# Attention on one core: one cell in five gets its exp on VectorE from 16-bit integer bits and a quadratic, with q, k and v cast and transposed by DMA, in a planned fixed order

## The chip, the cores and the metric

One core of a Trainium2 chip. The time is the device time of that core in microseconds (us). Most executions of one kernel agree within 0.3%. Each run has a state, fast or slow. A kernel's run carries runs of the kernel before on the same chip, so that ratios are taken within one chip.

Engines in the profile: PE is TensorE's matmuls, PEld its weight loads, DVE is VectorE, ACT is ScalarE, POOL is GpSimd, SP is the engine that only issues DMAs. A name with a q (SPq, POOLq) is that engine's issuing side.

## The reference

```python
# q [8, 8, 1024, 64], k and v [8, 2, 1024, 64], float32, all normal x 0.1
for g in range(2):                              # 4 query heads share a k, v head
    scores = (1/8) * q_group @ k_group.transpose(0, 1, 3, 2)
    attn = exp(scores - max(scores))
    attn = attn / (sum(attn) + 1e-08)
    output[:, 4*g : 4*g + 4] = attn @ v_group
```

The scores are tiny, so both kernels leave the maximum out. The sum comes from a column of ones beside v. Work is counted in cells of 128 keys by 512 queries: 8 batches x 8 heads x 2 query blocks x 8 key blocks are 1024 cells.

## The kernel before

Three cells make a wave: three score matmuls fill a PSUM tile of 1536 columns, and one ACTIVATE takes the exp of all. q and k are transposed by PE, and DVE copies the transposes out.

```python
def score_wave(gw, qT, kT):
    ...
    sps = spool.tile([128, CPERW, QBS], FP32, name="spsum")      # CPERW = 3, bufs=2
    for slot, gc in enumerate(cells):
        nc.tensor.matmul(sps[:, slot, :], lhsT=kT[b][g][side][:, c, :],
                         rhs=qT[(b, pair)][...], start=True, stop=True)
    pt = pT_pool.tile([128, CPERW, QBS], BF16, name="pt")
    nc.scalar.activation(out=pt[:, 0:n, :], in_=sps[:, 0:n, :], func=AF.Exp, scale=scale)
    return pt

def output_block(b, pair, side, qb, pts, vt):
    ...                          # 4 x 8 matmuls of pt by v and its column of ones
    nc.vector.reciprocal(out=rec, in_=ops[:, :, D])
    nc.vector.tensor_tensor(out=ost, in0=ops[:, :, 0:D], in1=rec..., op=ALU.mult)
    ...                          # DMA to out
```

The softmax here doesn't subtract the row's maximum and nothing guards it: scores larger than these inputs give would overflow.

## Time and profile before

| | before |
|---|---|
| time | 480.44 us, median of 2 runs (479.61 to 481.26) |
| ACT busy | 460.2 us of a span of 480.1 (96%) |
| PE busy / DVE busy / POOL busy | 443.3 / 129.3 / 141.1 us |
| granted PE clock, mean | 0.998 |

A high busy share does not make a bound by itself; who waits for whom does. The prediction below reads that from the groups, the chain of waits and the spacing of instructions, with their lines. One view that it only counts with is that of the DMA queues (packets, MB, share of 16 engines' span):

```profile
q1 hardware_dynamic: 102656, 25.18, 24.8%
q0 software_dynamic: 7168, 16.79, 11.1%
```

### The profile page before, as it was taken

The numbers are of one execution on the slowest core, as the hardware profiler recorded it, in microseconds if no ns is written. First come the engines' busy times: TensorE is split into PE (matmuls) and PEld (weight loads), VectorE is DVE, ScalarE is ACT, GpSimd is POOL, SyncE is SP. The second block draws the span as 40 slices with busy tenths as digits, with TensorE's granted clock in tenths as the row PEclk, the third lists the DMA queues.
The fourth block names the chain that finished last, engine by engine and source line by source line (L and its number), as shares of the span: only waits on it lengthen the run. The fifth ranks groups of instructions, "written<-read, shape, count | busy, mean of one in ns | idle before, by whom it ended". The sixth has DMA issues, their size and how long they took to land.

```text
span 480.1 us, 13304 instructions
## 1 busy us (share of the span) xinstructions
PE 443.3 (92%) x5632; PEld 282.6 (59%) x5632; DVE 129.3 (27%) x400; ACT 460.2 (96%) x343; POOL 141.1 (29%) x198
## 2 busy tenths in 40 slices
PE   2999999999999999999999999999999998988895
PEld 1566666666666666666565656656565555555553
DVE  3332233232242323222241312313222111111112
ACT  1699999999999999999999999999999999999996
POOL 9993056128047111830138010111100111101011
PEclk9999999999999999999999999999999999999999
DMA  7997356138157122842148121211212111111111
GB/s 177 218 227 182 79 142 169 45 90 219 35 125 198 47 55 58 197 109 58 35 115 206 34 56 46 67 34 35 56 45 58 40 39 35 46 34 34 46 34 45
DMA packets 109883, 42.82 MB, mean 89 GB/s; under 512 B 105728, under 2 KB 105728, under 8 KB 109824
## 3 DMA queue, kind: packets, MB, share of 16 engines
q1 hardware_dynamic: 102656, 25.18, 24.8%
q0 software_dynamic: 7168, 16.79, 11.1%
q8 instruction: 44, 0.72, 0.6%
q14 instruction: 15, 0.12, 0.1%
HBM read 25.17 MB, written 16.78 MB: 87 GB/s over the span
## 4 chain that ended last, share of the span: by engine, by line
ACT 72%; PE 21%; issue 3%; POOL 1%; DMA 1%; DVE 1%; POOLq 0%
ACT pt L191 72%; PE spsum L183 13%; PE opsum L204 6%; PE tpsum L107 2%; POOL qstage L87 1%; DMA qstage<-in_q_dram 1%; DVE ost L216 0%; DVE xT L111 0%; DVE rec L214 0%; POOL ident masks.py:199 0%; POOL ident masks.py:197 0%; POOLq masks.py:199 0%; POOLq L277 0%
## 5 line engine op out<-in xcount | busy, mean ns | idle before, releaser
L191 ACT ACTIVATE pt<-spsum 128x1536 bf16<-128x1536 f32 x342 | 458.9, 1706 | 14.6 <-PE spsum L183 14.6
L183 PE MATMUL spsum<-xT 128*128 128x512 bf16 x1024 | 278.2, 380 | 23.5 <-ACT pt L191 19.0
L204 PEld LDWEIGHTS <-pt 128*128 128x128 bf16 x4096 | 174.0, 98 | 75.9 <-DVE ost L216 16.9
L204 PE MATMUL opsum<-vstage,pt 128*128 128x65 bf16 x4096 | 191.1, 195 | 1.1 <-DVE ost L216 1.0
L183 PEld LDWEIGHTS <-xT 128*128 128x128 bf16 x1024 | 98.5, 97 | 94.2 <-issue 35.8
L222 POOL DMA_DIRECT2D out_dram<-ost x64 | 48.3, 755 | 316.1 <-DVE ost L216 283.6
L214 DVE RECIPROCAL rec<-opsum 128x4 f32<-128x4 f32 x128 | 23.4, 183 | 309.2 <-PE opsum L204 300.4
L87 POOL DMA_DIRECT2D qstage<-in_q_dram x128 | 92.2, 723 | 18.4 <-PE tpsum L107 12.8
L216 DVE TENSOR_TENSOR ost<-opsum,rec 128x256 f32<-128x256 f32 x128 | 53.8, 421 | 3.7 <-DVE rec L214 0.2
L111 DVE COPY xT<-tpsum 128x1024 bf16<-128x1024 bf16 x64 | 43.6, 681 | 32.9 <-PE tpsum L107 20.7
L107 PE MATMUL tpsum<-ident,kstage 128*128 128x128 bf16 x256 | 28.5, 226 | 5.4 <-DMA kstage<-in_k_dram 5.3
L107 PE MATMUL tpsum<-ident,qstage 128*128 128x128 bf16 x256 | 27.4, 225 | 3.3 <-DVE xT L111 1.6
L107 PEld LDWEIGHTS <-kstage 128*128 128x128 bf16 x256 | 18.9, 101 | 14.0 <-issue 5.7
L107 PEld LDWEIGHTS <-qstage 128*128 128x128 bf16 x256 | 18.6, 101 | 9.8 <-issue 2.8
L77 DVE MEMSET kstage<- 128x192 f32 x64 | 13.5, 218 | 2.3 <-PE tpsum L107 0.9
L191 ACT ACT_TABLE_LOAD x1 | 1.3, 1283 | 0.7 <-PEq L277 0.7
L96 DVE MEMSET vstage<- 128x8 f32 x16 | 0.9, 65 | 0.0
masks.py:199 POOL TENSOR_SCALAR_AFFINE_SELECT ident<-ident 128x128 bf16<-128x128 bf16 x1 | 0.3, 307 | 0.1
masks.py:197 POOL MEMSET ident<- 128x128 bf16 x1 | 0.2, 205 | 0.3 <-POOLq L277 0.3
L277 POOL MEMSET const-float32-0.0<- 128x1 f32 x1 | 0.1, 99 | 0.2 <-issue 0.2
L277 POOL MEMSET const-bfloat16-1.0<- 128x1 bf16 x1 | 0.1, 102 | 0.0
L277 POOL MEMSET const-uint8-127<- 128x1 uint8 x1 | 0.1, 102 | 0.0
(1 smaller groups left out, 0.1 us busy)
## 6 DMA issues: line engine op xcount, KB each, us to landing
qstage<-in_q_dram POOLq DMA_DIRECT2D x128, 64.0 KB, 3.7
qstage<-in_q_dram SPq DMA_DIRECT2D x128, 64.0 KB, 3.4
out_dram<-ost SPq DMA_DIRECT2D x64, 128.0 KB, 1.9
out_dram<-ost POOLq DMA_DIRECT2D x64, 128.0 KB, 2.3
kstage<-in_k_dram SPq DMA_DIRECT2D x64, 64.0 KB, 2.7
vstage<-in_v_dram SPq DMA_DIRECT2D x16, 256.0 KB, 3.1
```

What stands on the lines that cost most here:

```text
L77: nc.vector.memset(ks[:, 0::2, :], 0.0)
L87: eng.dma_start(out=qstage[sc][:, 2 * j : 2 * j + 2, :], in_=q[b, 2 * j : 2 * j + 2].rearrange("h (sc p) d -> sc p h d", p=128)[sc],)
L96: nc.vector.memset(vs[:, :, D], 1.0)
L107: nc.tensor.transpose(tp[:, sc, :], _hi16(stages[sc])[:, lo : lo + 2, :], ident)
L111: nc.vector.tensor_copy(out=dst, in_=tp)
L183: nc.tensor.matmul(sps[:, slot, :], lhsT=kT[b][g][side][:, c, :], rhs=qT[(b, pair)][:, qb * NQS : (qb + 1) * NQS, :], start=True, stop=True,)
L191: nc.scalar.activation(out=pt[:, 0:n, :], in_=sps[:, 0:n, :], func=AF.Exp, scale=scale)
L204: nc.tensor.matmul(ops[:, qs, :], lhsT=pts[gc // CPERW][:, gc % CPERW, qs * 128 : (qs + 1) * 128], rhs=_hi16(vt[b][g][:, c, :]), start=(c ...
L214: nc.vector.reciprocal(out=rec, in_=ops[:, :, D])
L216: nc.vector.tensor_tensor(out=ost, in0=ops[:, :, 0:D], in1=rec.unsqueeze(2).to_broadcast([128, NQS, D]), op=ALU.mult,)
L222: (nc.gpsimd if (qb + side) % 2 else nc.sync).dma_start(out=out[b, h].rearrange("(qs p) d -> p qs d", p=128)[:, qb * NQS : (qb + 1) * NQS, :],
L277: nc = _bacc.Bacc("TRN2", target_bir_lowering=False, num_devices=1)
```

## The change

ACT was the bound, so the change takes work from it. Four things are done together.

1. 194 of the 1024 cells go to DVE. A copy out of PSUM scales the score and adds 127 x 256, into a 16-bit integer. Its bits, shifted right by one, are those of a bf16 near exp; a quadratic in the low 8 bits corrects it. That is one step per cell and five steps for each group of four cells.
2. The other cells stay on ACT in pieces of two cells (1024 columns), not three, as PSUM banks are now needed for DVE's cells.
3. q and k are cast to bf16 by a DMA from DRAM to DRAM, issued by GpSimd, and read back by transposing DMAs that SP issues. GpSimd casts v, and copies k's halves into place.
4. A small simulation orders all instructions, with durations as its constants; no scheduler moves them.

```diff
+def make_plan(nj, nkc):
+    QK, PV, EXP, P1, NORM = 0.214, 0.142, 0.925, 0.665, 0.64
+    CHAIN = (0.60, 0.60, 1.08, 0.60, 1.08)
+    LIVE_A, LIVE_D, PENDING = 24, 7, 8
+    ...              # always takes the op that can start first; a cell goes to DVE when
+    ...              # a DVE bank is free before an ACT tile, with at most 8 pending
+            if pending < PENDING and (cur or live["D"] < LIVE_D):
+                td = max(pe, min(bank))
...
+def cast(key, src):
+    scr = scr_pool.tile([S, G * D], BF16, name="scr")        # in DRAM, bufs=4
+    nc.gpsimd.dma_start(out=scr..., in_=src...)
+    scratch[key] = scr
+def transpose(key, dst, n):
+    nc.sync.dma_start_transpose(out=dst[:, rows], in_=scratch[key][rows, :])
...
+# exp_bits, one cell, PSUM -> pd (uint16):   pd = score * bits_scale + 256*127
+# exp_curve, a group of four cells (2048 columns):
+#   z = pd & 0xFF            tensor_scalar
+#   y = z * A/512 + B/2      tensor_scalar, f16
+#   y = z * y                tensor_tensor
+#   z = pd >> 1              tensor_scalar
+#   pd = z + y               tensor_tensor, read as bf16
...
+            at(t0 - 24.0, cast, ("k", b), k[b])
+                at(t0 - 12.0 + 0.7 * n, transpose_k, b, n)
+                at(t0 - 5.0 + g, place_k, b, g)
...
+                at(max(tj - 21.0, -1.0), cast, ("q", b, j), q[b, j::NPAIR])
+                at(tj - 7.0 + 0.7 * n, transpose_q, b, j, n)
```

t0 and tj are the planned first use of a batch or a pair of heads, in us.

## The prediction

> **What bounds the kernel now.** I read the busy shares first, then the costliest groups, then the chain of waits, and last the timeline of each engine, for the spacing of its instructions. First the page's first part, and the stretches of the run.
>
> ```profile
> PE 443.3 (92%) x5632; PEld 282.6 (59%) x5632; DVE 129.3 (27%) x400; ACT 460.2 (96%) x343; POOL 141.1 (29%) x198
> ...
> 220.00:320.00 100.00, 95.31 (x1228) 60.87 (x1228) 26.78 (x81) 100.00 (x75) 22.05 (x30) 1.00 0.29 74
> ```
>
> PE and ACT both look full. Over 100 us of the middle (busy us of PE, weight load, DVE, ACT, POOL, then clock, DMA share, GB/s) ACT is busy for exactly 100. Who waits for whom decides between them:
>
> ```profile
> L191 ACT ACTIVATE pt<-spsum 128x1536 bf16<-128x1536 f32 x342 | 458.9, 1706 | 14.6 <-PE spsum L183 14.6
> L183 PE MATMUL spsum<-xT 128*128 128x512 bf16 x1024 | 278.2, 380 | 23.5 <-ACT pt L191 19.0
> L204 PE MATMUL opsum<-vstage,pt 128*128 128x65 bf16 x4096 | 191.1, 195 | 1.1 <-DVE ost L216 1.0
> ...
> ACT 72%; PE 21%; issue 3%; POOL 1%; DMA 1%; DVE 1%; POOLq 0%
> ```
>
> ACT idles 14.6 us behind the score matmuls in the whole run, 11.8 of them in one piece at the start, while PE waits for ACT all through. The kernel is ACT's exp over 1024 cells (a cell is 128 keys by 512 queries), plus a start and an end. Spacing, from the timeline of each engine (start, length):
>
> ```profile
> 228.88 12.47 ACT L191 ACTIVATE pt<-spsum 128x1536 bf16<-128x1536 f32 x9
> ...
> 232.00 0.81 PE L183 MATMUL spsum<-xT 128*128 128x512 bf16 x3 [0.27 <-ACT pt L191]
> 232.64 0.73 PE L204 MATMUL opsum<-vstage,pt 128*128 128x65 bf16 x17
> ...
> 11.92 2.72 PE L183 MATMUL spsum<-xT 128*128 128x512 bf16 x6 [0.78 <-DVE xT L111]
> ...
> 231.76 0.18 DVE L214 RECIPROCAL rec<-opsum 128x4 f32<-128x4 f32 x1 [3.35 <-PE opsum L204]
> 231.98 0.42 DVE L216 TENSOR_TENSOR ost<-opsum,rec 128x256 f32<-128x256 f32 x1
> ```
>
> - ACT: nine exps last 12.47 us; less one length of 1.71, over 8, they start every 1.345 us. The records overlap, so the mean length of 1706 ns is not the cost. 342 x 1.344 is 460 us of the 480.
> - PE: three score matmuls take 0.81, the last one 0.38, so they start every 0.215 us. Seventeen output matmuls take 0.73, the last 0.195: every 0.0335 us. PE's own need is 1024 x 0.215 + 4096 x 0.0335 = 220 + 137 = 357 us, not the 443 "busy". At the start six take 2.72: about 0.427 apart, half speed, up to about 20 us.
> - DVE: a reciprocal and the multiply after it take 0.22 + 0.42 = 0.64 us, 128 times: 82 us.
>
> **What the Trainium skill says.**
> - "ScalarE: Activation LUTs", What ACT_TABLE_LOAD costs: an ACTIVATE with immediate scale and bias takes 186 ns + 0.833 ns per element, and neighbours overlap by about 93. That makes 1373 ns between starts at 1536 elements; this trace has 1345. Keeping the slope, the fixed part is 1345 - 1280 = 65 ns, so an exp of 1024 should come every 853 + 65 = 0.918 us.
> - "VectorE: DVE Perf Modes", The perf-mode tier table: at 2048 elements of 16 bits in SBUF, a single-source operation takes 693 ns, tensor_tensor 1224; an fp32 PSUM source runs at one element per cycle. The trace has only the last kind: 0.42 us for 256 elements is 267 ns at 0.96 GHz plus 0.155.
> - "SBUF — State Buffer", Who interferes with whom: VectorE in a two-port mode and GpSimd exclude each other for a whole instruction, and a two-input VectorE instruction excludes GpSimd's reads. The kernel before cannot show it.
> - "TensorE: Matmul & The Clock Gate", What you observe: the first matmuls go at half speed. The 0.427 against 0.215 us agrees.
>
> **The change, part by part.** I counted instructions in the built program.
>
> *Exp leaves ACT.* 830 cells stay, as 415 exps of 1024; 194 go to DVE. ACT: 415 x 0.918 = 381 us, 79 less. Smaller pieces cost it: 277 pieces of 1536 would need 372. It also needs a quick PE. The old records give the round trip: the exp ends about 1.09 us after its start when not overlapped (1.45 less 512 x 0.833 = 1.02, plus 0.07 until PE starts), two matmuls 0.215 + 0.38, 0.04 to ACT: about 1.72. Two exps last 1.836. The slack is 0.11 us, less than one cell of output matmuls (4 x 0.0335 = 0.134), so I expect small gaps, 5 to 10 us in all: about 388.
>
> *DVE gets it.* Per group of four cells: 4 copies out of PSUM (512 elements, fp32 to 16 bits): 533 + 155 = 0.69 alone, some 0.66 where neighbours overlap: 2.64 us. Then three single-source steps and two tensor_tensor over 2048. The skill's lengths would be 0.69 and 1.22, the change's own planning constants are 0.60 and 1.08. Those constants look measured: 0.64 for the reciprocal and multiply and 0.214 for a score matmul both match the old trace. I lean to them, but each step waits for the one before: 0.63 and 1.12. Group: 2.64 + 3 x 0.63 + 2 x 1.12 = 6.77 us; 194 / 4 = 48.5 groups: 328. With the normalising, 82, DVE needs **410 us** (403 with the constants; 430 with the skill's lengths, 2.64 + 2.07 + 2.44 = 7.15 a group).
>
> *PE.* 512 transposes in the loop go (56 us busy in the groups, though pipelined); 16 stay at the start. 357 us of need remains.
>
> *Data.* Loads now go through a cast to DRAM by the GpSimd queue and a transposing DMA by the SP queue, issued some 21 and 7 us ahead. The old hardware queue had 102,656 packets in 24.8% of 16 engines' span: 0.248 x 480 x 16 / 102,656 = 18.5 ns each. The new kernel has about 65,500 output, 20,500 plain load, 77,800 cast and 38,900 transposed rows: 202,700 x 18.5 ns / 16 = 235 us, an estimate, if these rows cost the same. That fits beside the rest.
>
> *Sum.* So DVE (410) is now the longest, ACT (388) and PE (357) close behind, and the fixed order ties them: DVE's late group holds PE, and PE holds ACT. Start: k and q of the first pair are 1 MB; the old start moved 177 to 227 GB/s in its slices, so about 5 us after 1.5 of issue, shared with v and a cast: 8.5; cast, 8 cold transposes, a copy and a score matmul bring DVE's first piece to about 13. End: from the last multiply to the end, 2.8 now, 3 later. Cold PE and port collisions: 2. Total 410 + 13 + 3 + 2 = **428 us**, 11% less.
>
> **The rivals.**
> 1. *ACT stays the bound.* For: it was; 381 plus gaps. Then DVE would show idle time and the run would be 388 + 13 + a tail of one group's steps and the last outputs, near 10: 411. Against: DVE's 403 even by its most favourable durations.
> 2. *DVE is much slower.* If the bit operations or mixed 16-bit types miss the fast modes: five steps at 2048/0.96 = 2.13 us make a group 13.3 us and DVE 727: far slower than before. Against: all operands are 16 bits, contiguous, in SBUF. With the skill's lengths and full waits: 430 + 18 = 448.
> 3. *GpSimd blocks DVE.* 32 copies on GpSimd, of 512 or 1024 elements, perhaps 0.6 to 1 us each; DVE is in steps that exclude it about half of the time: up to 13 us more, 441.
> 4. *Data comes late.* If cast rows cost much more than 18.5 ns, PE waits at each new batch or pair; 31 pairs follow the first, so 1 us each is 459. For: DRAM to DRAM in pieces of 128 bytes is nothing the old kernel did. Against: 21 us of lead.
>
> **Range and chances.** Rival 1 sets the low edge, 412; the slow ends of 2 and 3 the high edge, 450. Faster by over 2% needs less than 470.8: 0.94. Within 2%: 0.04, a late-data case. Slower: 0.02, the missed fast modes.
>
> **What would show it.** DVE busy above 93% and ACT near 90%; exps every 0.918 us where unhindered; single-source steps at 0.60 to 0.69 and tensor_tensor at 1.08 to 1.22; PE's waits for DVE pd, not for DMA; score matmuls 0.215 apart after the start; first exp near 13 us. Wrong if steps are 1 us or more, if PE waits for transposed tiles, or if DVE idles while ACT is full.

## The result, and the profile after

| | before | after |
|---|---|---|
| time | 480.44 us | 449.15 us, median of 2 runs (447.18 to 451.13) |
| ratio | 1 | 0.9351 (95%: 0.9246 to 0.9455) |
| ACT busy | 460.2 | 389.7 (87%) |
| DVE busy | 129.3 | 416.8 (93%) |
| PE busy | 443.3 | 386.4 (86%) |
| granted PE clock | 0.998 | 0.979 |

A ratio is the mean time of one kernel's fast runs over that of the other's of the same rounds, so not quite the ratio of the medians. Later four more runs on another chip gave a median of 449.4 (444.32 to 452.32), ratio 0.9307: the result stands.

The kernel is 6.5% faster, not 11%. First the page of the kernel after: the busy shares, the DMA queues, the chain of waits by engine, and four groups (busy us, mean ns | idle before, releaser).

```profile
PE 386.4 (86%) x5136; PEld 234.2 (52%) x5136; DVE 416.8 (93%) x699; ACT 389.7 (87%) x417; POOL 111.3 (25%) x80
...
q1 hardware_dynamic: 132160, 32.01, 39.2%
q0 software_dynamic: 78432, 9.96, 37.5%
...
DVE 55%; PE 20%; DMA 9%; ACT 6%; issue 6%; SPq 3%; POOL 1%; ACTq 0%; POOLq 0%; DVEq 0%
...
L335 ACT ACTIVATE pa<-aps 128x1024 bf16<-128x1024 f32 x415 | 387.4, 1044 | 32.5 <-PE aps L324 30.5
...
L344 DVE TENSOR_SCALAR pd<-dps 128x512 uint16<-128x512 f32 x194 | 126.0, 682 | 6.3 <-PE dps L324 6.2
...
L395 PE MATMUL ops<-vset,pd 128*128 128x65 bf16 x776 | 38.2, 195 | 24.0 <-DVE pd L387 23.5
L248 POOL DMA_DIRECT2D scr<-in_q_dram x31 | 77.8, 2948 | 0.0
```

The bound has moved from ACT (72% of the old chain, 6% of this one) to DVE (1%, now 55%). PE waits for DVE's last step (pd, 23.5 us), and ACT then waits for PE's scores (30.5 us). Two lines are surprising. The DMA queues fill 77% of 16 engines' span, not 52% (235 us of 449). And an issue of a cast holds GpSimd for about 2 us: the records of queued issues overlap, so their mean of 2948 ns says too much, but one ends every 2.03 us. L248 is no transfer: q's data land a median of 7.8 us after the issue. I call it the writing of descriptors (the orders for the single pieces of a transfer), after the Trainium skill's page on SBUF that is named at the end; the runs show when GpSimd is busy with an issue, not what it does in it.

Next the lengths of DVE's steps, each line's own view in the kernel after (shortest/median/longest in ns), and below it the mean of the same lines from the groups with shapes kept apart.

```profile
L359 DVE TENSOR_SCALAR z<-pd x49: 420/684/2250, 19.1 to 441.5; 128x2048 uint16<-128x2048 uint16 x48, 128x1024 uint16<-128x1024 uint16 x1
...
L365 DVE TENSOR_SCALAR y<-z x49: 428/684/2112, 20.9 to 442.0; 128x2048 f16<-128x2048 uint16 x48, 128x1024 f16<-128x1024 uint16 x1
```

```profile
L375 DVE TENSOR_TENSOR y<-z,y 128x2048 f16<-128x2048 uint16 x48 | 60.9, 1268 | 1.7
L387 DVE TENSOR_TENSOR pd<-z,y 128x2048 uint16<-128x2048 uint16 x48 | 59.6, 1242 | 1.5
L359 DVE TENSOR_SCALAR z<-pd 128x2048 uint16<-128x2048 uint16 x48 | 39.7, 826 | 0.0
L365 DVE TENSOR_SCALAR y<-z 128x2048 f16<-128x2048 uint16 x48 | 39.2, 818 | 0.4
L377 DVE TENSOR_SCALAR z<-pd 128x2048 uint16<-128x2048 uint16 x48 | 35.7, 743 | 1.7
```

A step with a mean of 826 ns, a median of 684 and a longest of 2250 is not slow: it is a fast step that is now and then held. The medians of the five, in the order of the table, are 1226, 1226, 684, 684 and 694 ns. The means stand 42, 16, 142, 134 and 49 ns above them; the sum, 383 ns, times 48 groups is **18.4 us**. (The copies out of PSUM, 674 to 692 ns, are never held.) What holds the five is seen where GpSimd's timeline is laid beside DVE's (start, length). DVE, an undisturbed stretch and then a held one:

```profile
207.75 0.68 DVE L359 TENSOR_SCALAR z<-pd 128x2048 uint16<-128x2048 uint16 x1
208.47 0.69 DVE L365 TENSOR_SCALAR y<-z 128x2048 f16<-128x2048 uint16 x1
209.19 1.22 DVE L375 TENSOR_TENSOR y<-z,y 128x2048 f16<-128x2048 uint16 x1
...
277.42 2.25 DVE L359 TENSOR_SCALAR z<-pd 128x2048 uint16<-128x2048 uint16 x1
...
280.13 1.69 DVE L365 TENSOR_SCALAR y<-z 128x2048 f16<-128x2048 uint16 x1
281.85 1.23 DVE L375 TENSOR_TENSOR y<-z,y 128x2048 f16<-128x2048 uint16 x1
```

GpSimd beside the held stretch, nothing but issues of casts:

```profile
277.16 4.02 POOL L248 DMA_DIRECT2D scr<-in_q_dram  x2
279.17 4.11 POOL L248 DMA_DIRECT2D scr<-in_k_dram  x1
280.31 5.00 POOL L248 DMA_DIRECT2D scr<-in_q_dram  x1
```

At 207.75, with GpSimd idle (its timeline has nothing from 202 to 210), the steps take 0.68, 0.69 and 1.22 us. Beside the four issues of casts the first two take 2.25 and 1.69; the tensor_tensor takes 1.23 and is not held. Over the whole run 28 of the 240 full steps are held by more than 50 ns: 12 of them, with 10.0 us, lie beside issues of casts alone, 10 with 5.9 us beside issues and GpSimd's own copies, and 6 with 2.6 us beside copies alone. The 188 steps with GpSimd idle all stay within 11 ns of their medians. The kinds differ: beside issues alone 12 of 17 single-source steps are held and none of 12 tensor_tensor steps; beside a copy a tensor_tensor is held too (1.94 us at 218.78).

The waits of the kernel after (who, for whom: us in total, times, longest):

```profile
PEld L395 <- DVE pd L387: 42.2, 41, 3.1
...
ACT pa L335 <- PE aps L324: 30.5, 42, 2.3
...
PE aps L324 <- DMA qT<-scr: 5.1, 3, 2.1
PEld L324 <- POOL kset L265: 5.1, 4, 2.0
```

PE waits mostly for DVE, but also for q and k: late data is there. Part of its path is SP's queue, whose issues follow one another in its timeline: a transposing DMA takes SP about 1.23 us to issue (four in 4.96), and an output that waits for DVE's normalising (143 us of waits in that queue, 73.2 for the multiply and 70.0 for the reciprocal) stands before the transposes behind it. How much of the lateness that makes was not measured. After a wait PE is slow as well. In the timeline of PE in the kernel after:

```profile
77.41 0.60 PE L324 MATMUL aps<-qT,kset 128*128 128x512 bf16 x2 [2.11 <-DMA qT<-scr]
...
79.00 1.06 PE L324 MATMUL dps<-qT,kset 128*128 128x512 bf16 x2
```

Two score matmuls usually take 0.59 to 0.60; from 78.3 to about 82 they take up to 1.06, as slow as at a cold start. The clock record of the trace agrees: it grants 0.5 for 3.41 us from 78.52 and again from 119.48. Another 12.3 us at 0.5 lie after 433.5, where the work runs out; together they make the mean clock of 0.979.

**The account.** In the profiled run DVE takes its first cell at 13.77 us, and its last work ends at 446.1. Between these are 432.3 us: 18.4 of holding, 8.6 of idle time in gaps over 0.06 us, and the rest, 405.3, undisturbed work with the hand-overs between steps (0.03 us each). The medians from start to start give the same 405: 48.5 groups of 6.91 us and 128 normalisings of 0.55. With 3.1 us for the last output that is 13.8 + 405.3 + 18.4 + 8.6 + 3.1 = 449.2.

### The profile page after: what moved, and what is told of

Read it like the earlier page. It is cut to its first block, busy times and chain, and to the rows that moved or that the text cites. A ratio compares the mean times of both kernels' runs of the same rounds, so it can differ in the third digit from the quotient of the medians.

```text
span 449.2 us, 12594 instructions
## 1 busy us (share of the span) xinstructions
PE 386.4 (86%) x5136; PEld 234.2 (52%) x5136; DVE 416.8 (93%) x699; ACT 389.7 (87%) x417; POOL 111.3 (25%) x80
## 3 DMA queue, kind: packets, MB, share of 16 engines
q0 software_dynamic: 78432, 9.96, 37.5%
## 4 chain that ended last, share of the span: by engine, by line
DVE 55%; PE 20%; DMA 9%; ACT 6%; issue 6%; SPq 3%; POOL 1%; ACTq 0%; POOLq 0%; DVEq 0%
DVE pd L344 11%; DVE y L375 10%; DVE pd L387 9%; PE aps L324 9%; DMA qT<-scr 7%; PE ops L395 6%; DVE ost L410 6%; DVE y L365 6%; ACT pa L335 6%; DVE z L377 5%; PE dps L324 4%; DVE z L359 4%; DVE rec L408 3%; SPq L256 2%; DMA kT<-scr 1%
## 5 line engine op out<-in xcount | busy, mean ns | idle before, releaser
L335 ACT ACTIVATE pa<-aps 128x1024 bf16<-128x1024 f32 x415 | 387.4, 1044 | 32.5 <-PE aps L324 30.5
L324 PE MATMUL aps<-qT,kset 128*128 128x512 bf16 x830 | 250.0, 383 | 21.3 <-ACT pa L335 11.4
L395 PEld LDWEIGHTS <-pa 128*128 128x128 bf16 x3320 | 137.0, 99 | 65.1 <-DVE ost L410 11.5
L395 PE MATMUL ops<-vset,pa 128*128 128x65 bf16 x3320 | 145.7, 195 | 3.0 <-DVE ost L410 3.0
L344 DVE TENSOR_SCALAR pd<-dps 128x512 uint16<-128x512 f32 x194 | 126.0, 682 | 6.3 <-PE dps L324 6.2
L324 PEld LDWEIGHTS <-kset 128*128 128x128 bf16 x1024 | 85.6, 98 | 85.4 <-issue 41.8
L248 POOL DMA_DIRECT2D scr<-in_q_dram x31 | 77.8, 2948 | 0.0
L324 PE MATMUL dps<-qT,kset 128*128 128x512 bf16 x194 | 65.2, 386 | 2.4 <-DMA qT<-scr 1.1
L375 DVE TENSOR_TENSOR y<-z,y 128x2048 f16<-128x2048 uint16 (+1 forms) x49 | 61.6, 1257 | 1.7
L395 PEld LDWEIGHTS <-pd 128*128 128x128 bf16 x776 | 32.1, 98 | 52.0 <-DVE pd L387 42.2
L395 PE MATMUL ops<-vset,pd 128*128 128x65 bf16 x776 | 38.2, 195 | 24.0 <-DVE pd L387 23.5
L359 DVE TENSOR_SCALAR z<-pd 128x2048 uint16<-128x2048 uint16 (+1 forms) x49 | 40.1, 818 | 0.0
L377 DVE TENSOR_SCALAR z<-pd 128x2048 uint16<-128x2048 uint16 (+1 forms) x49 | 36.1, 736 | 1.7
L248 POOL DMA_DIRECT2D scr<-in_k_dram x7 | 28.6, 4079 | 0.0
(12 smaller groups left out, 10.6 us busy)
```

Source lines behind the costliest of these rows:

```text
L248: nc.gpsimd.dma_start(out=scr.rearrange("s (g d) -> s g d", g=G), in_=src.rearrange("g s d -> s g d"),)
L324: nc.tensor.matmul(dst, lhsT=ksets[b % 2][:, g, c * 128 : (c + 1) * 128], rhs=qT[(b, j)][:, qb * QBS : (qb + 1) * QBS], start=True, stop=True,
L335: nc.scalar.activation(out=pt[:, 0:m], in_=psum.pop(("A", n))[:, 0:m], func=AF.Exp, scale=scale)
L344: nc.vector.tensor_scalar(out=groups[g][:, slot], in0=psum.pop(cell), scalar1=bits_scale, scalar2=bits_bias, op0=ALU.mult, op1=ALU.add,)
L359: nc.vector.tensor_scalar(out=z, in0=pd, scalar1=0xFF, scalar2=None, op0=ALU.bitwise_and)
L375: nc.vector.tensor_tensor(out=y, in0=z, in1=y, op=ALU.mult)
```

## The experiments

The theory after the result: DVE is the bound, and GpSimd's writing of cast descriptors holds its steps. The rivals: the copies on GpSimd hold them; late data costs the time; the smaller exps or the round trip between PE and ACT cost it. The medians are of all four runs, of which one is slow in the changed kernel's second set, in e2 and in e10. The kernel before ran beside each batch, with medians of 481.5, 481.6 and 481.3 us.

| run | median us (4 runs) | ratio (95%) | DVE busy | ACT idle after 13 us (gaps over 0.15 us) |
|---|---|---|---|---|
| changed kernel, again | 449.4 | 0.9307 (0.9241 to 0.9372) | 418.8 | 29.3 |
| e1, no casts | 434.25 | 0.9033 (0.8999 to 0.9067) | 403.6 | 14.1 |
| e2, casts unread | 446.82 | 0.9253 (0.922 to 0.9286) | 415.3 | 26.8 |
| e3, no copies | 451.3 | 0.9374 (0.9336 to 0.9412) | 411.2 | 32.1 |
| e4, every exp on ACT | 490.82 | 1.0192 (1.0173 to 1.0212) | 80.5 | 0.7 |
| e5, data early | 446.83 | 0.9286 (0.9253 to 0.932) | 415.0 | 25.3 |
| e6, 184 cells on DVE | 441.06 | 0.9171 (0.9134 to 0.9208) | 401.4 | 19.3 |
| e7, 176 cells | 446.47 | 0.9262 (0.9214 to 0.9309) | 389.1 | 24.5 |
| e8, 176 cells, data early | 426.26 | 0.886 (0.8834 to 0.8885) | 387.1 | 3.2 |
| e9, 172 cells, data early, end on ACT | 419.27 | 0.8719 (0.8697 to 0.8742) | 380.3 | 2.9 |
| e10, every cast twice | 473.2 | 0.9795 (0.9759 to 0.9831) | 427.4 | 51.5 |

### e1 and e2: the casts away, and the casts there but unread

e1 casts once and reads that tile for all q and k:

```diff
 def cast(key, src):
+    if "fixed" in scratch:
+        scratch[key] = scratch["fixed"]
+        return
...
-    scratch[key] = scr
+    scratch[key] = scratch["fixed"] = scr
```

> Wrong result on purpose: every transposing DMA reads the first cast pair's scratch, so only 1 of the 38 casting DMAs of the GpSimd queue is issued. Theory P (port): the casts' descriptor writing on GpSimd blocks VectorE's fast steps; expects the means of the steps z (L359) and y (L365) to fall from 818 and 810 ns to about 690, VectorE's busy time from 416.8 to about 402 us, and the time from 449 to about 432. Theory L (late data): the loss is PE waiting for transposed q; expects the DMA waits of PE to shrink and a similar gain, but the step means may stay. Theory S (steps are simply longer than predicted): time stays at 447 to 450.

e2 makes all casts, into tiles that nobody reads:

```diff
-    scr = scr_pool.tile([S, G * D], BF16, name="scr")
+    pool = scr_pool if "fixed" in scratch else fixed_pool
+    scr = pool.tile([S, G * D], BF16, name="scr")
...
-    scratch[key] = scr
+    scratch[key] = scratch.setdefault("fixed", scr)
```

> Wrong result on purpose: the casts are issued as in the changed kernel, but into scratches that nobody reads; the transposing DMAs read the first one and wait for no cast. Theory P expects the step means to stay near 815 ns and the time near 446 to 449; theory L (late because of the casts) expects the same gain as the run without casts, about 432.

Both work with wrong q and k on purpose. They still passed the tolerance, as scores this small make nearly equal weights; this says nothing for their results, and it means that a "right result" below shows little about q and k. The same two groups of e1, then of e2:

```profile
L368 DVE TENSOR_SCALAR y<-z 128x2048 f16<-128x2048 uint16 x48 | 33.5, 698 | 0.4
L362 DVE TENSOR_SCALAR z<-pd 128x2048 uint16<-128x2048 uint16 x48 | 33.0, 688 | 0.0
```

```profile
L369 DVE TENSOR_SCALAR y<-z 128x2048 f16<-128x2048 uint16 x48 | 39.1, 814 | 0.4
L363 DVE TENSOR_SCALAR z<-pd 128x2048 uint16<-128x2048 uint16 x48 | 38.7, 807 | 0.0
```

Without casts the means fall to 698 and 688, close to the median of 684; with casts that nothing waits for they are back at 814 and 807. The casts as work cost 10.6 us by the ratios (12.6 by the medians), and DVE's busy time differs by 11.7. Whether it is GpSimd's issuing or the transfers, the two runs alone do not tell; the packets in the trace of the changed kernel do. 17 of its 28 held steps have no packet of the casts' queue in flight, and of the steps with GpSimd idle 41 have those packets in flight (over 0.3 of 16 engines) and none is held. So the transfers are not what holds DVE. Waiting for the casts costs little: e2 is 2.6 us faster than the changed kernel, and their intervals overlap.

### e3: the copies on GpSimd away

```diff
-            for g in range(G):
-                at(t0 - 5.0 + g, place_k, b, g)
+            if b == 1:
+                for g in range(G): at(t0 - 5.0 + g, place_k, b, g)   # place_v alike
```

> Wrong result on purpose: GpSimd's own copies of k and v into their padded tiles stop after the second batch (24 of 30 go). Theory P with the descriptors as the blocker expects at most 3 to 4 us: 445 to 447. Rival: GpSimd's copies are the blocker, as the prediction's third rival had it: then 10 to 13 us go and the time is about 437.

The result is wrong on purpose (relative error 1.24). DVE's busy time fell by 5.6 us, yet the time did not fall. With nothing on GpSimd to hold them the casts ran ahead; all were issued by 136.9 us, and their traffic delayed the transposes: from 55 to 140 us one landed a median of 6.8 us after its issue, against 3.2 in the changed kernel. From the waits:

```profile
PE aps L324 <- DMA qT<-scr: 15.8, 6, 8.9
```

Neither expectation came. The experiment changed two things, and does not price the copies in time. In DVE's steps it does: they stand 12.8 us above their medians, 5.6 less than before. e1 agrees: there the casts are gone and the copies left, and the means of the five steps stand only 5.9 us in total above the medians (48 x 122 ns).

### e4: every exp on ACT

```diff
-    LIVE_A, LIVE_D, PENDING = 24, 7, 8
+    LIVE_A, LIVE_D, PENDING = 24, 7, 0
```

> One part undone: all 1024 cells get exp on ACT, in 512 pieces of 1024; loads, order and the rest as in the changed kernel. If ACT's pace of 0.918 us holds: 470 us plus about 13 at the start and 5 to 8 at the end: 488 to 492, slower than the kernel before. If ACT loses slots to the shorter pieces (PE's round trip of about 1.72 of 1.836 us), over 495.

The timeline of ACT in e4:

```profile
194.67 50.81 ACT L335 ACTIVATE pa<-aps 128x1024 bf16<-128x1024 f32 x55
```

Less one length of 1.085, over 54, the exps start every 0.921 us. 512 of them are 471 us, against 460 in pieces of 1536: without DVE's share the change costs 1.9%. DVE's share alone is worth 490.8 - 449.4 = 41 us (two batches, by the medians). It also answers a step of mine: ACT idles for 0.7 us in gaps over 0.15 us, and 1.5 in all, so the round trip between PE and ACT leaves no gap even with two PSUM tiles. My 5 to 10 us of small gaps do not exist.

### e5: data early

```diff
-scr bufs=4;  q: cast tj-21, transposes tj-7;   k: cast t0-24, transposes t0-12, place_k t0-5
+scr bufs=6;  q: cast tj-33, transposes tj-19;  k: cast t0-40, transposes t0-26, place_k t0-12
```

> Same work and right result; only the data come earlier: casts 12 to 16 us ahead of where they stood, the transposing DMAs 12 to 14, GpSimd's k copies 7; six scratches in place of four. Theory L (late data): PE's waits for transposed q and placed k (17 us in all) vanish; as VectorE is the bound, only its own 8.6 us of waits can come back: 441 to 446. Theory P alone: within 2 us of the changed kernel, 447 to 451.

PE no longer waits for qT or kset at all, and DVE's waits fall to 4.8 us. The time fell by 1.0 us by the ratios (2.6 by the medians), and the intervals overlap (0.9253 to 0.932 against 0.9241 to 0.9372); it lies between the two ranges expected. Late data is real, and nearly hidden while DVE is the bound.

### e6 and e7: the plan with measured lengths

The plan trusted the short steps of its constants, and so gave DVE too much. e6 gives it the measured means; e7 also keeps longer lengths for the copy and the normalising. The plan then sends 184 and 176 cells to DVE.

```diff
-    QK, PV, EXP, P1, NORM = 0.214, 0.142, 0.925, 0.665, 0.64
-    CHAIN = (0.60, 0.60, 1.08, 0.60, 1.08)
+    QK, PV, EXP, P1, NORM = 0.214, 0.142, 0.918, 0.60, 0.55      # e7: ... 0.66, 0.60
+    CHAIN = (0.84, 0.86, 1.30, 0.78, 1.16)                       # e7: ... 1.20
```

> Only the planning constants are changed, to what VectorE's steps took in the trace with the blocking in it; the plan then gives VectorE 184 cells in place of 194. Theory: VectorE is the bound and a cell costs it about 1.8 us (334 us of unblocked steps and 19 of blocking, over 194), ACT gets 5 more exps of 0.918: VectorE's busy time 416.8 - 18 = 399 us, time 449 - 18 = 431 (428 to 435). Rival (ACT or PE is as much the bound as VectorE): 445 to 450.

> Same, with constants that give VectorE 176 cells. VectorE's need falls by 33 us to about 384, ACT's rises to 424 x 0.918 = 389 plus its gaps; so ACT becomes the bound and the gain is smaller than 33: 389 + 13 at the start + 8 at the end + 10 of gaps: about 420 (416 to 428). Rival: the fixed order makes PE's waits for late data the bound, 435 or more.

e6 gained 8 us, not the 18 I expected. e7 missed by 26: DVE needs 28 us less than in the changed kernel, and the time is 3 us lower. Its waits from 14 to 440 us say why:

```profile
DVE rec L408 <- PE ops L395: 30.8, 39, 4.0
...
PE aps L324 <- DMA qT<-scr: 12.6, 5, 4.1
...
PEld L324 <- POOL kset L265: 7.1, 4, 3.3
```

Now DVE waits for PE (30.8 us), and PE for q and k. With DVE lighter, late data is the new bound.

### e8 and e9: both together, and the end

If that is so, e5's leads must pay in e7 what they did not pay alone. e8 is e7 with e5's leads. e9 also sends the last 24 cells to ACT, since in the changed kernel the last exp ends at 431.3 and 18 us of DVE's steps and output matmuls follow it.

```diff
-            if pending < PENDING and (cur or live["D"] < LIVE_D):
+            if nxt < n - 24 and pending < PENDING and (cur or live["D"] < LIVE_D):   # e9
```

> VectorE gets 176 cells as in e7, and the data come as early as in e5; right result. In e7 the bound had moved: PE waited some 25 us for transposed q and placed k, and ACT had 24.5 us of gaps. Theory: with the lighter VectorE the late data are the bound, so earlier data give most of that back: ACT 395 busy, gaps under 8, start 12.5, 14 after the last exp: 425 to 432. Rival: the gaps come from PE's order or from GpSimd's blocking: 440 to 446.

> As e8, and the last 24 cells all go to ACT (172 cells on VectorE in all), so that no group of four is left for VectorE when ACT is done. From e8: the 14 us between the last exp and the end fall to about 6, ACT gets two exps more (1.8 us): 419 to 426, 5 to 7 below e8. Rival: the end stays 13 us long, then no gain or 2 us worse.

e8: 426.26, 20 us less than e7 for the same edit that gave 1 to 3 by itself. e9: another 7, **419.27 us**, 6.7% under the changed kernel's median (6.3% by the ratios, as the two ran on different chips), with a right result. Its page, and the chain by engine:

```profile
PE 371.4 (89%) x5052; PEld 231.6 (55%) x5136; DVE 380.3 (91%) x647; ACT 395.0 (95%) x428; POOL 109.5 (26%) x80
...
ACT 70%; DVE 15%; issue 7%; PE 5%; DMA 2%; SPq 0%; ACTq 0%; DVEq 0%
```

ACT is the bound again, with DVE close. The granted clock is 1.0: after the start PE waits at most 1.0 us for DVE at once (3.1 in the changed kernel), and at most 0.3 for a transposed tile (2.1).

### e10: every cast twice

```diff
+    idle = idle_pool.tile([S, G * D], BF16, name="idle")
+    nc.gpsimd.dma_start(out=idle..., in_=src...)         # the same cast again, unread
```

> The suspected cost doubled: the changed kernel with every cast issued twice, the second into a scratch nobody reads. Theory P: VectorE's busy time grows by about what taking the casts away saved, 13.6 us (416.8 to about 430), the time by 12 or more (462 or more; the second casts also load the DMA engines, which may make data late and add to it). Rival (descriptor writing is not what blocks): VectorE's busy time stays at 415 to 419.

```profile
L373 DVE TENSOR_SCALAR y<-z 128x2048 f16<-128x2048 uint16 x48 | 43.5, 906 | 0.4
L367 DVE TENSOR_SCALAR z<-pd 128x2048 uint16<-128x2048 uint16 x48 | 42.7, 889 | 0.0
```

688, 807 and 889 ns for the first step with no casts, the casts once and twice: the holding grows with the casts. Over the five steps it is 5.9, 17.3 and 27.4 us in total. DVE's busy time grew by 10.6 us over the profiled result, about what the first set costs. The time grew by 24; the rest goes with late data, as PE's wait for qT is 13.7 us in place of 5.1, and DVE's waits are 21.2.

## Why the prediction was right or wrong

The direction and the range (412 to 450) held, the range by luck: the median of 449.15 lies 0.85 us inside its edge, the profiled run (451.13) outside it, and that edge had been set by rivals 2 and 3 (448 and 441), neither of which came as described. The central 428 was 21 us short. The sums redo, but for two roundings (430 is 428.8, 235 is 234.4) and one reading: the old trace does have another PSUM source than fp32, the copy xT<-tpsum in bf16. Step by step:

- **The bound before, and ACT's new need.** Right. The exps start every 0.921 us in e4 where I had 0.918. The gaps of 5 to 10 us were wrong: e4 has 0.7. ACT's 29.4 us of idle time in the changed kernel come from DVE and late data, through PE.
- **DVE, 410 us.** Right in sum, by two errors that cancel. From start to start the single-source steps take 0.67, 0.72 and 0.73 where I had 0.63, and the two tensor_tensor 1.26 and 1.14 (the next instruction overlaps its end) where I had 1.12; but the copies come every 0.60, not 0.66, and a reciprocal and its multiply overlap their neighbours and take 0.55, not 0.64. By the account it is 405. I leaned on the change's planning constants for the chain because two others matched the old trace; they were short by about a sixth with the hand-over, by an eighth without, and the lengths that I quoted from the Trainium skill, "VectorE: DVE Perf Modes" (0.69, 1.22), were right. The normalising had been read off the old trace where nothing stood next to it.
- **Start 13, end 3.** Right: 13.8 and 3.1.
- **"Cold PE and port collisions: 2."** This is the term that failed. It measured 18.4 us of holding plus 8.6 of DVE's waits, 27 in all. 13.8 + 405.3 + 27.0 + 3.1 is 449.2.
- **Rival 3, GpSimd blocks DVE.** Right in its mechanism, wrong in its agent. I counted 32 copies (the trace has 30) and up to 13 us, and put it in the high edge alone. The casts were in my list of parts, but only as transfers: I never asked what it costs GpSimd to write their descriptors. That is 77.8 us of its time (k's records, 28.6 us, lie inside q's), and most of the holding: 18.4 us with the casts, 5.9 without (e1).
- **Data, "235 us ... fits beside the rest".** Wrong by half: 52% of 16 engines estimated, 77% measured. A row of the casts is not a row of the old loads: 37.5% of 449.2 x 16 us over 78,432 packets is 34 ns each, not 18.5. Rival 4 was therefore there, as waits of PE for qT and kset, but hidden behind DVE until e7 uncovered it.
- **Rivals 1 and 2.** ACT did not stay the bound, and no step missed the fast lengths.
- **What was to be seen.** DVE at 93% and ACT at 87% came nearly as written, and PE waited chiefly for pd; but a sign of being wrong showed too, 6.2 us of PE's waits for transposed q. Single-source medians of 684 to 694 lie at the upper end of what I gave; tensor_tensor's 1226 is just above it.

How the 8.6 us of waits divide between late data, half-speed matmuls and the plan's order stays open; e5 bounds the first at a few us. Of the 18.4 us of holding, the 5.9 beside both issues and copies cannot be divided.

## What to carry to other kernels

When work moves onto an engine, list not only its instructions but what shares its memory ports, and count the DMA issues of GpSimd as instructions of GpSimd with their own length. Compare the mean with the median of a step: where they differ, look at what the other engine did in the long ones. And after taking load off a bound, try again what did not pay before: the earlier loads gave 1 to 3 us alone and 20 once DVE was lighter.

## What the Trainium skill lacked or had wrong

- "SBUF — State Buffer", its box on DVE and software descriptors, tells of one direction: DVE keeps GpSimd from writing descriptors. Here the other one cost the time: GpSimd's writing held single-source steps from 0.68 to as much as 2.25 us, 10.0 us beside issues of casts alone. Its section Who interferes with whom does say that whichever issues first blocks the other, and the held steps agree.
- "TensorE: Matmul & The Clock Gate", What's actually happening, puts the return to half speed after an idle window of about 3.4 us. Here a wait of 2.11 us was followed by half speed for 3.41 us.
- "DMA: Bandwidth & Descriptors", Anatomy of one DMA, calls the generation of descriptors on GpSimd's path small and variable, without a figure. Here a cast of q's pair or of k, 2048 rows of 128 bytes, kept GpSimd for 2.03 us.
- No page that I read gives what the issue of a transposing DMA of 256 rows costs SP's queue (1.23 us here).
